# Spreading the places of the split weight strips by 32 bytes in a decoder-layer kernel

## The chip, the cores and the metric

One core of one Trainium2 chip runs the whole kernel. The metric is the device time of one execution in microseconds; the time before is the median of three runs.

## The reference

One decoder layer on 1024 tokens of width 1024, all in float32: a feed-forward half-step, a mixer with three branches, a second feed-forward half-step, each with a norm before and after. Cut to the matrix products that fill the time:

```python
f1 = swiglu(rms_norm(h, ffn1_pre_g), ffn1_w_in, ffn1_w_out)      # 1024 -> 2 x 2816 -> 1024
h = h + 0.5 * rms_norm(f1, ffn1_post_g)
u = rms_norm(h, mix_pre_g)
p_rwkv, p_swa, q_mem, gate_logits = split(u @ w_in)              # 1024 -> 1792 + 768 + 512 + 3072
y_a, y_b, y_c = rwkv7_mix(...), sliding_window_gqa(...), memory_cross_attention(...)
merged = g_a * (y_a @ w_branch[0]) + g_b * (y_b @ w_branch[1]) + g_c * (y_c @ w_branch[2])
h = h + rms_norm(merged @ w_out, mix_post_g)
f2 = swiglu(rms_norm(h, ffn2_pre_g), ffn2_w_in, ffn2_w_out)
return h + 0.5 * rms_norm(f2, ffn2_post_g)
```

## The kernel before

Activations lie feature-major: 128 features on the partitions, 512 tokens (one half) along them, in tiles of 2048 bytes per partition. A product of two float32 numbers is made of three matmuls in the type float32r: each operand is split into a rounded part, hi, and the rest, lo, and mm3 adds hi x hi, hi x lo and lo x hi in PSUM. The weight is the operand that is loaded into TensorE (stationary), the activations stream past it (moving). Every matmul comes with a weight load of its own, also where two that follow each other use the same weights.

The weights come in strips, in the order of a list that plan() writes. Half a strip is four blocks of 128 x 128, 2048 bytes per partition. raw() sends the DMA of a half into one of five w_raw buffers; operand() makes w_hi of it on ScalarE (a cast) and w_lo on VectorE (a subtraction). In the feed-forward input layers the halves are also added and subtracted first (w_sum and the raw buffers in operands()), since these layers use a scheme with fewer products on sums of blocks. prefetch() runs this eight operands ahead of the matmuls, at a raised priority; a recording layer orders the instructions of each engine by readiness and priority, and the DMAs of the weights keep their program order on SyncE's queue. For the last strips of the second feed-forward layer, operand() takes a pool of its own, keep.

w_hi and w_lo each have eight buffers (OPS) of 2048 bytes. Where they lie follows from the pools: the constants end at byte 17632 of a partition, the five raw buffers at 27872; the eight hi places start at 27872 + 2048 i, the eight lo places at 44256 + 2048 i. Divided by 512 all sixteen leave the remainder 224. The blocks inside a place are 512 bytes apart. The moving operands: the u tiles start at 163808 + 2048 i, the f and r tiles at 108512 + 2048 i, all with remainder 480; the y tiles of the last branch (line 379 and 380 write them) at 60640 + 2048 i, remainder 224; the keep pool's places have remainder 480. Of the float32 matmuls outside mm3, mkv against mem_g have remainders 224 and 224 (line 1023), bones against m 480 and 256 (line 820).

The lines of mm3 are 317, 318 and 319; operand()'s cast is line 254 and its subtraction 256. px, py, pz, po, pgate, pr, pq, pb and pw name PSUM tiles by what they hold; px, py and pz are those of the feed-forward inputs.

Of the kernel before, what the change touches and what calls it, by code (L numbers as in the profile page):

```python
# [11 lines left out]
F32R = mybir.dt.float32r  # L12
# [5 lines left out]
P = 128  # L18
# [17 lines left out]
OPS = 8  # L36
# [164 lines left out]
class Builder:  # L201
# [4 lines left out]
    def plan(self):  # L206
        seq = []
        for f in ("ffn1", "ffn2"):
            items = [(f + "_gate", j) for j in range(FIRST[f])] + [(f + "_rest", j) for j in range(FIRST[f])]
            items += [(f + "_pair", j) for j in range(FIRST[f], KF)]  # L210
            items += [(f + "_out", q) for c in OUT_STRIPS for q in c]

            items += [(f + "_out", q) for q in OUT_STRIPS[-1]] * (f == "ffn1")
            if f == "ffn1":
                seq += items
                first = [("win", f) for f in MIX_FIRST]
                seq += first + [("win", f) for f in FILL] + first
                seq += [("win", f) for p in range(NPAIR) for f in (8 + p, 4 + p, p) if f not in MIX_FIRST]
                seq += [("win", j) for j in ATT_BLOCKS]
                seq += [("win", 24 + g) for g in range(24)]  # L220
                seq += [("wb", 4 * i + q) for i in BRANCHES + BRANCHES[2:] for q in range(4)]
                seq += [("wout", o) for o in range(KD)] * 2
            else:
                seq += items
        self.seq = seq
        self.raws = []
        for name, i in seq:
            f, _, kind = name.partition("_")
            if kind in ("gate", "rest", "pair"):
                self.raws += [(f + "_in", i)] + [(f + "_in", i + KF)] * (kind != "gate")  # L230
            else:
                self.raws.append((name, i))
        self.raw_pos, self.raw_ready = 0, []
        self.lead, self.urgent = 300, 1000
        self.op_base = self.op_use = self.op_pos = 0
        self.ops_ready = []
        self.gen = self.operands()

    def raw(self, ahead):
# [9 lines left out]
        return self.raw_ready.pop(0)  # L249

    def operand(self, x, pool=None):
        pool = pool or self.wpool
        hi = pool.tile([P, 4, P], F32R, tag="w_hi", name="w_hi", bufs=OPS)
        self.nc.scalar.copy(hi, x)  # L254
        lo = pool.tile([P, 4, P], F32R, tag="w_lo", name="w_lo", bufs=OPS)
        self.nc.vector.tensor_tensor(lo, x, hi.bitcast(F32), ALU.subtract)  # L256
        return hi, lo

# [1242 lines left out]
```

## Time and profile before

| | |
|---|---|
| median of three runs | 2378.07 us (2376.53 to 2379.35) |
| the profiled execution | 2381.53 us, span 2379.8 us |
| mean granted TensorE clock | 0.996 |
| HBM read and written | 231.41 and 89.13 MB |

By stage (windows of the span, busy us of the engine in it):

| us | what runs | PE | DVE | ACT |
|---|---|---|---|---|
| 0 to 200 | start, first part of ffn1's input layer | 189.56 | 156.61 | 84.91 |
| 200 to 460 | rest of it | 260.00 | 146.54 | 98.20 |
| 460 to 790 | ffn1's output layer, first projections | 328.21 | 213.95 | 117.85 |
| 790 to 1220 | the recurrence and projections beside it | 427.40 | 304.06 | 156.90 |
| 1220 to 1530 | attention, gates, branches | 305.65 | 169.66 | 142.55 |
| 1530 to 1680 | last branch, output projection | 146.53 | 99.68 | 59.16 |
| 1680 to 2100 | ffn2's input layer | 419.06 | 304.61 | 163.13 |
| 2100 to 2380 | ffn2's output layer and the end | 267.48 | 148.32 | 68.94 |

A row of the profile names the line, the engine, the operation, and output <- inputs with buffer numbers left out; PE is a matmul, PEld a weight load. Busy time of PE counts overlapping matmuls once. A row of the timeline gives start and duration in us. A row of windows gives the stretch, its length, busy us (and instructions) by engine in the order PE, PEld, DVE, ACT, POOL where they occur, the granted clock, the DMA share and GB/s. A row of waits says who waited for whom: us in total, times, the longest.

### The profile page before, as it was taken

The numbers are of one execution on the slowest core, as the hardware profiler recorded it, in microseconds if no ns is written. First come the engines' busy times: TensorE is split into PE (matmuls) and PEld (weight loads), VectorE is DVE, ScalarE is ACT, GpSimd is POOL, SyncE is SP. The second block draws the span as 40 slices with busy tenths as digits, with TensorE's granted clock in tenths as the row PEclk, the third lists the DMA queues.
The fourth block names the chain that finished last, engine by engine and source line by source line (L and its number), as shares of the span: only waits on it lengthen the run. The fifth ranks groups of instructions, "written<-read, shape, count | busy, mean of one in ns | idle before, by whom it ended". The sixth has DMA issues, their size and how long they took to land.

```text
span 2379.8 us, 33514 instructions
## 1 busy us (share of the span) xinstructions
PE 2343.9 (98%) x12388; PEld 1916.1 (81%) x12388; DVE 1543.4 (65%) x2584; ACT 891.6 (37%) x1648; POOL 95.5 (4%) x134
## 2 busy tenths in 40 slices
PE   8999999999999999999999999999999999999998
PEld 6788888888888777888868887778888888878888
DVE  6986555655478776894655456475998765564535
ACT  5423333422345444223454455234652233342211
POOL 0000000000000000001310000240000000000000
PEclk9999999999999999999999999999999999999999
DMA  7453222533244325325444324555545432263303
GB/s 277 136 188 121 86 87 80 178 115 106 97 161 142 110 99 189 135 93 175 144 156 153 123 97 150 185 188 166 174 162 183 156 120 82 83 202 100 114 23 107
DMA packets 196195, 323.80 MB, mean 136 GB/s; under 512 B 35360, under 2 KB 65568, under 8 KB 195776
## 3 DMA queue, kind: packets, MB, share of 16 engines
q1 hardware_dynamic: 180000, 294.33, 37.7%
q10 hardware_dynamic: 16032, 27.33, 3.4%
q8 instruction: 98, 1.61, 0.3%
q14 instruction: 65, 0.53, 0.1%
HBM read 231.41 MB, written 89.13 MB: 135 GB/s over the span
## 4 chain that ended last, share of the span: by engine, by line
PE 89%; DVE 5%; DMA 3%; ACT 2%; issue 1%; ACTq 0%; SPq 0%; DVEq 0%
PE po L317 7%; PE po L318 6%; PE po L319 6%; PE px L317 6%; PE px L318 6%; PE px L319 6%; PE pgate L317 4%; PE pgate L319 4%; PE pgate L318 4%; PE pz L317 3%; PE pz L318 3%; PE pz L319 3%; PE pr L319 2%; PE pr L317 2%; PE pr L318 2%; PE pb L318 2%
## 5 line engine op out<-in xcount | busy, mean ns | idle before, releaser
L254 ACT CAST w_hi<-w_raw 128x512 fp32r<-128x512 f32 x544 | 336.6, 621 | 903.0 <-PE po L318 213.1
L256 DVE TENSOR_TENSOR w_lo<-w_raw,w_hi 128x512 fp32r<-128x512 f32 x544 | 381.5, 702 | 183.0 <-ACT w_hi L254 171.7
L317 PE MATMUL po<-u,w_hi 128*128 128x512 f32 (+1 forms) x768 | 285.9, 372 | 0.9 <-DVE acc L627 0.9
L318 PE MATMUL po<-u,w_hi 128*128 128x512 f32 (+1 forms) x768 | 285.3, 372 | 0.0
L319 PE MATMUL po<-u,w_lo 128*128 128x512 f32 (+1 forms) x768 | 285.3, 372 | 0.0
L630 DVE TENSOR_TENSOR acc<-po,acc 128x512 f32<-128x512 f32 (+1 forms) x136 | 89.6, 658 | 162.6 <-PE po L319 162.0
L317 PEld LDWEIGHTS po<-u,w_hi 128*128 128x128 f32 x768 | 144.7, 188 | 26.3 <-DVE acc L627 1.6
L318 PEld LDWEIGHTS po<-u,w_hi 128*128 128x128 f32 x768 | 144.7, 188 | 24.9
L319 PEld LDWEIGHTS po<-u,w_lo 128*128 128x128 f32 x768 | 144.7, 188 | 25.0
L317 PE MATMUL pgate<-u,w_hi 128*128 128x512 f32 x384 | 152.8, 398 | 0.0
L319 PE MATMUL pgate<-u,w_lo 128*128 128x512 f32 x384 | 151.8, 395 | 0.0
L318 PE MATMUL pgate<-u,w_hi 128*128 128x512 f32 x384 | 150.0, 391 | 0.0
L317 PE MATMUL px<-f,w_hi 128*128 128x512 f32 x352 | 137.6, 391 | 3.1 <-ACT u L543 0.9
L317 PE MATMUL px<-u,w_hi 128*128 128x512 f32 x352 | 137.3, 390 | 1.2 <-ACT vm L1110 0.9
L318 PE MATMUL pz<-u,w_hi 128*128 128x512 f32 x352 | 137.2, 390 | 0.2 <-DVE u L380 0.2
L319 PE MATMUL px<-u,w_lo 128*128 128x512 f32 x352 | 137.2, 390 | 0.0
L317 PE MATMUL pz<-u,w_hi 128*128 128x512 f32 x352 | 137.0, 390 | 0.1
L319 PE MATMUL pz<-u,w_lo 128*128 128x512 f32 x352 | 137.0, 389 | 0.0
L318 PE MATMUL px<-u,w_hi 128*128 128x512 f32 x352 | 137.0, 389 | 0.0
L318 PE MATMUL px<-f,w_hi 128*128 128x512 f32 x352 | 136.9, 389 | 0.0
L319 PE MATMUL px<-f,w_lo 128*128 128x512 f32 x352 | 136.9, 389 | 0.0
L389 ACT ACTIVATE sq<-acc 128x512 f32<-128x512 f32 (+1 forms) x104 | 61.0, 598 | 93.2 <-DVE acc L630 75.7
(314 smaller groups left out, 4665.7 us busy)
## 6 DMA issues: line engine op xcount, KB each, us to landing
w_raw<-in_ffn_in SPq DMA_DIRECT2D x220, 256.0 KB
w_raw<-in_win SPq DMA_DIRECT2D x112, 256.0 KB
w_raw<-in_ffn_out SPq DMA_DIRECT2D x104, 256.0 KB
hid_d<-g SPq DMA_DIRECT2D x88, 256.0 KB
hid<-hid_d SPq DMA_DIRECT2D x88, 256.0 KB
gate_d<-gate SPq DMA_DIRECT2D x24, 512.0 KB
pk_d<-pk ACTq DMA_DIRECT2D x4, 2560.0 KB
f<-pk_d SPq DMA_DIRECT2D x16, 640.0 KB
```

What stands on the lines that cost most here:

```text
L254: self.nc.scalar.copy(hi, x)
L256: self.nc.vector.tensor_tensor(lo, x, hi.bitcast(F32), ALU.subtract)
L317: mm(out, wh, xh, start=first, stop=False, **kw)
L318: mm(out, wh, xl, start=False, stop=False, **kw)
L319: mm(out, wl, xh, start=False, stop=last, **kw)
L389: nc.scalar.activation(sq, x, ACT.Square)
L630: self.nc.vector.tensor_tensor(out, ps, out, ALU.add)
```

## The change

Each of the sixteen places gets a buffer name of its own, with one buffer of 4 x 128 + 8 numbers, 2080 bytes, of which the first 2048 are used. plan() asks for all of them at the start, hi first, so that they lie one behind the other; operand() takes them in turn (place), hi and lo together, ahead of the cast. The keep pool goes on as it was.

```diff
+        self.place = 0
+        for t in ("hi", "lo"):
+            for i in range(OPS):
+                self.wpool.tile([P, 4 * P + 8], F32R, tag=f"w_{t}{i}", name=f"w_{t}", bufs=1)
...
     def operand(self, x, pool=None):
-        pool = pool or self.wpool
-        hi = pool.tile([P, 4, P], F32R, tag="w_hi", name="w_hi", bufs=OPS)
+        if pool:
+            hi, lo = (pool.tile([P, 4, P], F32R, tag="w_" + t, name="w_" + t, bufs=OPS) for t in ("hi", "lo"))
+        else:
+            hi, lo = (
+                self.wpool.tile([P, 4 * P + 8], F32R, tag=f"w_{t}{self.place}", name=f"w_{t}", bufs=1)[:, : 4 * P].rearrange("p (k c) -> p k c", c=P)
+                for t in ("hi", "lo")
+            )
+            self.place = (self.place + 1) % OPS
         self.nc.scalar.copy(hi, x)
-        lo = pool.tile([P, 4, P], F32R, tag="w_lo", name="w_lo", bufs=OPS)
         self.nc.vector.tensor_tensor(lo, x, hi.bitcast(F32), ALU.subtract)
```

In the built program the hi places now start at 17632 + 2080 i and the lo places at 34272 + 2080 i: remainders 224, 256, 288, 320, 352, 384, 416, 448 and 480, 0, 32, 64, 96, 128, 160, 192. The raw buffers lie behind them at 50912 + 2048 i (remainder 224, as before). Everything behind in the left part of the memory moves up by 512 bytes; the u, f, r and hid tiles, which are laid from the right, stay.

The number of instructions of each engine is unchanged. Their order differs at three places: the first pairs of ffn1's input layer, a few projections of the mixer, and the first pairs of ffn2's input layer. ScalarE's queue in the first pairs of ffn1, before (w_sum and w_raw are the sources of the split, u and f parts of the moving operands, g the gate):

```order
L254 CAST w_hi<-w_raw 128x512
L254 CAST w_hi<-w_sum 128x512
L379 CAST u<-acc 128x512
L254 CAST w_hi<-w_raw 128x512
L379 CAST f<-t 128x512 x3
L254 CAST w_hi<-w_raw 128x512 x2
L558 ACTIVATE g<-g 128x512 x2
L254 CAST w_hi<-w_raw 128x512
L254 CAST w_hi<-w_sum 128x512
```

and in the changed program (ten lines were added above, so that line 254 is 265, 379 is 389, 558 is 568):

```order
L265 CAST w_hi<-w_raw 128x512
L389 CAST u<-acc 128x512
L389 CAST f<-t 128x512
L265 CAST w_hi<-w_sum 128x512
L389 CAST f<-t 128x512 x2
L265 CAST w_hi<-w_raw 128x512 x2
L568 ACTIVATE g<-g 128x512
L265 CAST w_hi<-w_sum 128x512
L265 CAST w_hi<-w_raw 128x512 x4
```

The first split of w_sum comes later by two casts of moving operands, the second one earlier by one split and one activation. TensorE's queue at the same place, where groups of two pairs are interleaved (mm3's lines 317 to 319 are 327 to 329 in the changed program), before:

```order
L317 MATMUL px<-f,w_hi 128x512
L319 MATMUL px<-u,w_lo 128x512
L317 MATMUL px<-u,w_hi 128x512
L318 MATMUL px<-u,w_hi 128x512
L318 MATMUL px<-f,w_hi 128x512
L319 MATMUL px<-f,w_lo 128x512
L317 MATMUL px<-f,w_hi 128x512
```

and in the changed program:

```order
L327 MATMUL px<-f,w_hi 128x512 x2
L328 MATMUL px<-f,w_hi 128x512
L329 MATMUL px<-f,w_lo 128x512
L328 MATMUL px<-f,w_hi 128x512
L329 MATMUL px<-f,w_lo 128x512
L327 MATMUL px<-f,w_hi 128x512 x2
L328 MATMUL px<-f,w_hi 128x512 x2
```

The groups on u that stood between those on f have moved behind them; the matmuls are the same ones.

## The prediction

> **What bounds the kernel now.** I read the page first: how busy each engine is, and what the chain that ended last is made of.
>
> ```profile
> PE 2343.9 (98%) x12388; PEld 1916.1 (81%) x12388; DVE 1543.4 (65%) x2584; ACT 891.6 (37%) x1648; POOL 95.5 (4%) x134
> PE 89%; DVE 5%; DMA 3%; ACT 2%; issue 1%; ACTq 0%; SPq 0%; DVEq 0%
> ```
>
> TensorE is busy for 98% of the span and holds 89% of the chain. Next I asked for three stretches: the first 24 us, the last 14 us, and what lies between.
>
> ```profile
> 24.00:2366.00 2342.00, 2323.97 (x12301) 1899.00 (x12301) 1526.03 (x2535) 876.74 (x1622) 92.61 (x125) 1.00 0.41 134
> ```
>
> Between the two ends TensorE idles 2342.00 - 2323.97 = 18.0 us in all, at a granted clock of 1.00. So a change pays only if it alters the pace of the matmul stream itself; all stalls together are 18 us. The pace is read from the timeline, in a stretch with no stall, for a 512-column matmul on split weights and its weight loads, and later for the 256-column ones at the end:
>
> ```profile
> 299.66 0.39 PE L319 MATMUL py<-r,w_lo 128*128 128x512 f32 x1
> 299.89 0.39 PE L317 MATMUL py<-r,w_hi 128*128 128x512 f32 x1
> ...
> 301.93 0.39 PE L317 MATMUL px<-u,w_hi 128*128 128x512 f32 x1
> 299.89 0.19 PEld L318 LDWEIGHTS py<-r,w_hi 128*128 128x128 f32 x1
> 300.12 0.19 PEld L319 LDWEIGHTS py<-r,w_lo 128*128 128x128 f32 x1
> 2329.74 0.28 PE L319 MATMUL po<-u,w_lo 128*128 128x256 f32 x1
> ...
> 2331.18 0.28 PE L319 MATMUL po<-u,w_lo 128*128 128x256 f32 x1
> ```
>
> Columns are start, duration, engine, line, operation. The 0.39 is the latency of one matmul; they overlap, and the pace is the distance between starts. From 299.66 to 301.93 lie ten steps: 227 ns each. From 2329.74 to 2331.18 lie twelve: 120.0 ns each. So 256 more columns cost 107 ns, 0.417 ns a column; 512 columns are 213.4 ns, and **13.3 ns per matmul are fixed**, whatever its width. Each weight load (0.19 us) starts when the matmul ahead of it starts and is over before the next one is due. Whether the fixed part has to do with where the weights lie is the whole question.
>
> **The change part by part.** *The offsets.* All matmuls on split strips are at the three lines of mm3:
>
> ```profile
> 0.00:2380.00 2380.00, 1194.27 (x3088) 580.24 (x3088) 1.00 0.41 136
> 0.00:2380.00 2380.00, 1189.19 (x3088) 580.31 (x3088) 1.00 0.41 136
> 0.00:2380.00 2380.00, 1193.72 (x3088) 580.43 (x3088) 1.00 0.41 136
> ```
>
> These are the windows over the whole span for lines 317, 318 and 319 alone: 3 x 3088 = 9264 matmuls, each with a load. Their fixed part is 9264 x 13.3 ns = 123 us, 5.2% of the time. That is the most any placement could win, and each ns on all of them is 9.3 us.
>
> Before, all sixteen places leave the remainder 224 when the address is divided by 512, and the u, f and r tiles leave 480: the distance is 256 everywhere. The y tiles of the last branch, though, lie at remainder 224, a distance of 0. Their pace:
>
> ```profile
> 1565.77 0.39 PE L317 MATMUL pb<-y,w_hi 128*128 128x512 f32 x1
> ...
> 1567.13 0.39 PE L317 MATMUL pb<-y,w_hi 128*128 128x512 f32 x1
> ```
>
> Six steps in 1.36 us, 227 ns: the same. Within a strip the four blocks lie 512 bytes apart and run evenly through the rows of 299.66 to 301.93, so no multiple of 256 matters. What the trace lacks for these operands is a distance that is an odd multiple of 32. It has them for plain F32 matmuls, seen by their loads:
>
> ```profile
> L1023 PE MATMUL pq<-mkv,mem_g 128*128 128x512 f32 x32 | 14.1, 595 | 0.0
> 25.10 0.19 PEld L1023 LDWEIGHTS pq<-mkv,mem_g 128*128 128x128 f32 x1 [0.24 <-issue]
> ...
> 27.25 0.19 PEld L1023 LDWEIGHTS pq<-mkv,mem_g 128*128 128x128 f32 x1 [0.24 <-issue]
> 812.88 0.19 PEld L820 LDWEIGHTS rk<-m,bones 128*128 128x128 f32 x1 [0.24 <-issue]
> 813.31 0.19 PEld L820 LDWEIGHTS rk<-m,bones 128*128 128x128 f32 x1 [0.24 <-issue]
> 813.74 0.19 PEld L318 LDWEIGHTS pr<-u,w_hi 128*128 128x128 f32 x1 [0.24 <-issue]
> ```
>
> The mkv product is 16 matmuls in the program and 32 records here, so each record streams its columns twice: 5 steps in 2.15 us are 430 ns, which is 2 x 213.4 and 3 ns more. There weights and moving operand lie 0 apart. For rk<-m,bones they lie 288 apart (480 against 256; nine times 32), and the steps are 430 ns again. So where an odd distance can be seen, it costs and saves nothing. It is no proof: an F32 record takes twice as long for its columns, so its reads may have room that the split operands lack.
>
> Bounds: if nothing is read at a worse moment, 0; if the fixed part falls to the F32 rows' 3 ns on all matmuls, 9264 x 10.3 ns = 95 us faster; if all take the slowest undisturbed steps of this trace, dearer. I find those where the stream follows other matmuls:
>
> ```profile
> 814.40 0.19 PEld L317 LDWEIGHTS pr<-u,w_hi 128*128 128x128 f32 x1
> 814.63 0.19 PEld L318 LDWEIGHTS pr<-u,w_hi 128*128 128x128 f32 x1
> 814.87 0.19 PEld L319 LDWEIGHTS pr<-u,w_lo 128*128 128x128 f32 x1
> ```
>
> Steps of 235 ns, 8 above the steady 227: 9264 x 8 = 74 us slower. Between -95 and +74 I take **0**, since every distance that the rows do show, two for the split operands and an even and an odd one for F32, gives the same pace.
>
> The Trainium skill bears on the fixed part twice. "TensorE: Matmul & The Clock Gate", in its step-by-step part, says that loading the next weights takes no read bandwidth from the running matmul, since the two have ports of their own; by that rule no distance matters. The F32 rows agree (3 ns), the 13.3 ns need another reason. Its section "Back-to-back issue gap" gives N/2.4 + 2.5, 216 ns for 512 columns; by that figure 11 ns x 9264 = 101 us would be there to win. [...]
>
> *The writes into the places.*
>
> ```profile
> L254 ACT CAST w_hi<-w_raw 128x512 fp32r<-128x512 f32 x544 | 336.6, 621 | 903.0 <-PE po L318 213.1
> L256 DVE TENSOR_TENSOR w_lo<-w_raw,w_hi 128x512 fp32r<-128x512 f32 x544 | 381.5, 702 | 183.0 <-ACT w_hi L254 171.7
> ```
>
> The same casts and subtractions write into shifted places. Were each a tenth dearer (34 and 38 us), it would hide behind matmuls: ACT idles 903 us and DVE 183 us ahead of exactly these. I take 0.
>
> *The order.* No instruction is added or removed. With places of their own the scheduler puts the split of w_sum ahead of other splits in the first pairs of both feed-forward layers, and in ffn1 a block of three-matmul groups (f before u) moves with it. What can be won there is what stands idle:
>
> ```profile
> 100.00:170.00 70.00, 68.54 (x295) 54.53 (x295) 60.39 (x97) 23.06 (x41) 3.06 (x9) 1.00 0.51 164
> PE px L317 <- DVE u L541: 0.7, 2, 0.4
> PE px L317 <- ACT w_hi L254: 0.7, 2, 0.4
> 1790.00:1880.00 90.00, 89.54 (x395) 73.48 (x394) 70.26 (x112) 26.06 (x44) 0.00 (x0) 1.00 0.50 163
> ```
>
> The idle time is 1.46 us in ffn1's first pairs and 0.46 in ffn2's: at most 1.9 us faster. For a loss, a split that slips behind one other comes 0.62 + 0.70 = 1.3 us late; on each of the six pairs or so that the rows touch, it is 8 us. DVE is busy for 60.39 of 70 us there, so some slip is likely, yet the split moved forward is waited for as well; I take 0 and keep -2 to +8. If a split comes late, what waits is PE's next px group, and behind it the whole stream.
>
> *The size.* 512 bytes per partition more move the pools above by 512, a multiple of all that the distances above are counted in: 0.
>
> **Sum.** The profiled execution took 2381.5 us (span 2379.8 and 1.7 around it); 0 + 0 + 0 leaves it there. It is 3.5 us above the median of the three runs, 2378.07, so I forecast **2378 us** as a median, no change.
>
> **The rivals.**
>
> *The equal distance is what costs the 13.3 ns (faster).* For it: the fixed part is there although each load ends before its matmul, it is 4 times the F32 rows', and the one distance class is common to all places. Against: the y rows and the odd F32 rows. If half of the sixteen new distances were free, 9264/2 x 10.3 = 48 us: 2330; if all but one, 2290.
>
> *Some new distances collide (slower).* The loads run in step with the moving stream (rows at 299.89), so a shift of 32 bytes could put both onto the same part of the memory for the whole load. At half of the places and 8 ns, 37 us: 2415. It decides from one place in eight upward (9264/8 x 8 ns = 9 us). For it: nothing in the trace has tried such distances. Against: the F32 rows.
>
> *The order bites (slower).* The splits pulled forward delay the sums that the next pair needs: +5 to +8 us, 2384 to 2386.
>
> *The change doesn't do what it says.* It does: in the built program the hi places leave remainders 224, 256 ... 448 and the lo places 480, 0, 32 ... 192, sixteen different ones, against 480 of the u tiles. Only the operands of the last kept strips, in a pool of their own, stay as they are.
>
> **How the numbers follow.** About 0.2% (4.8 us) is what a measurement of this kernel can tell from no change. No change of pace: 0.52; faster by distance 0.24; collisions 0.16; order 0.08. The first case holds 2374 to 2383 and spills 0.02 to either side. Faster: 0.24 + 0.02 = 0.26. Within 0.2%: 0.48. Slower: 0.16 + 0.08 + 0.02 = 0.26. The likeliest case's own range is 2374 to 2383. For 8 in 10 the range must take in about half of both pace cases: down to 2328, just beyond the half-free case, and up to 2412, near the half-colliding one.
>
> **What would show it.** Right: steps of 227 and 120 ns in the same stretches, at every place; 18 us of idle time, give or take 3; the windows 100 to 170 and 1790 to 1880 with under 3 us of idle time more. Wrong by the first rival: steps below 227 ns that repeat with a period of eight strips' halves. By the second: steps above 227 with that period, and PE still 98% busy. By the third: waits of px for w_hi or w_lo above 2 us in the first pairs. The forecast is wrong as soon as steps differ between places by more than 0.5 ns on average.

## The result, and the profile after

The changed kernel takes **2415.9 us** (2414.35 to 2416.97, three runs) against 2378.07: 1.0156 times the time before, 95% interval 1.0142 to 1.017. The profiled execution took 2416.97 us, span 2415.2. One execution of e3, an experiment below, took 4759.84 us, about twice as long as the others; no run shows why, and e3's figures are those of its other three.

The page of the changed kernel: busy time by engine, and the chain that ended last (lines 317 to 319 of mm3 are 327 to 329 now).

```profile
PE 2385.2 (99%) x12388; PEld 1918.1 (79%) x12388; DVE 1544.4 (64%) x2584; ACT 894.7 (37%) x1648; POOL 95.6 (4%) x134
PE 92%; DVE 3%; DMA 2%; ACT 2%; issue 1%; DVEq 0%; ACTq 0%; SPq 0%
```

TensorE is busy for 41.3 us more with the same 12388 matmuls; the other engines have not changed by 4 us. The windows of the changed kernel, between the two ends and at the two places where the order changed (stretch, length, busy us and instructions of PE, PEld, DVE, ACT, POOL, granted clock, DMA share, GB/s):

```profile
24.00:2401.50 2377.50, 2365.08 (x12302) 1900.80 (x12302) 1526.90 (x2534) 879.76 (x1622) 92.70 (x125) 1.00 0.40 132
100.00:170.00 70.00, 69.08 (x295) 54.70 (x295) 60.28 (x97) 24.26 (x41) 3.19 (x9) 1.00 0.50 163
1813.00:1905.00 92.00, 92.00 (x398) 74.44 (x397) 71.08 (x113) 24.79 (x41) 0.00 (x0) 1.00 0.49 163
```

The waits of TensorE in ffn1's first pairs, and the groups that write into the places:

```profile
PE px L327 <- DVE u L551: 0.6, 1, 0.6
PE px L327 <- ACT w_hi L265: 0.3, 1, 0.3
```

```profile
L265 ACT CAST w_hi<-w_raw 128x512 fp32r<-128x512 f32 x544 | 337.2, 621 | 924.6 <-PE po L328 217.9
L266 DVE TENSOR_TENSOR w_lo<-w_raw,w_hi 128x512 fp32r<-128x512 f32 x544 | 381.4, 703 | 196.1 <-ACT w_hi L265 183.8
```

The two waits come to 0.9 us, against 1.4 before, and the splits take what they took. The idle time went down, from 18.0 to 2377.50 - 2365.08 = 12.4 us, and in the first pairs from 1.46 to 0.92 and from 0.46 to 0. The clock is the same. So the time was lost in the pace of the stream itself. The timeline of TensorE in the changed kernel (start, duration in us):

```profile
290.57 0.39 PE L329 MATMUL pz<-u,w_lo 128*128 128x512 f32 x1
290.80 0.39 PE L327 MATMUL px<-f,w_hi 128*128 128x512 f32 x1
...
293.07 0.39 PE L328 MATMUL px<-f,w_hi 128*128 128x512 f32 x1
293.30 0.40 PE L329 MATMUL px<-f,w_lo 128*128 128x512 f32 x1
293.53 0.39 PE L327 MATMUL pz<-u,w_hi 128*128 128x512 f32 x1
...
296.09 0.39 PE L329 MATMUL pz<-u,w_lo 128*128 128x512 f32 x1
296.32 0.40 PE L327 MATMUL px<-f,w_hi 128*128 128x512 f32 x1
...
298.89 0.39 PE L329 MATMUL px<-f,w_lo 128*128 128x512 f32 x1
```

Twelve matmuls use one pair of places. From 290.57 to 293.30 twelve steps take 2.73 us, 227.5 ns each; from 293.30 to 296.09 they take 2.79, 232.5 each; from 296.09 to 298.89 2.80, 233.3 each. The pace changes with the last matmul on the old place (293.30): that is the one under which the first weights of the next place are loaded.

The same in numbers of matmuls, in 260 us of ffn1 without a stall, before and then after:

```profile
200.00:460.00 260.00, 260.00 (x1149) 215.36 (x1148) 146.54 (x226) 98.20 (x167) 0.00 (x0) 1.00 0.28 94
```

```profile
200.00:460.00 260.00, 260.00 (x1123) 210.62 (x1122) 143.25 (x221) 94.29 (x159) 0.00 (x0) 1.00 0.25 86
```

1149 matmuls went through before, 1123 now. This row is the quickest way to read the pace and stands below for other kernels too.

Every matmul of the trace can be matched to the program, and so to the addresses of its moving operand and of the weights whose load runs beneath it, those of the next matmul. Mean steps of 512-column matmuls on split weights in the changed kernel, by the moving operand's address less that of the weights loaded beneath it, modulo 256 (steps of stalls, over 300 ns, left out; a thousand or more steps each):

```
distance     0     32     64     96    128    160    192    224
mean ns  227.2  233.2  230.0  233.6  232.2  233.6  233.2  233.1
```

All together the 8683 such steps average 231.98 ns, against 227.02 before (8685): 8683 x 4.96 ns = 43 us more. Less idle time gives 18.0 - 12.4 = 5.6 back; 37 are left, and the profiled executions differ by 35.4, the medians by 37.8. These are means: at the distance 96, for instance, the steps under which a lo part is loaded average 236.6 ns and the others 232.1.

### The profile page after: what moved, and what is told of

It is laid out like the page before. It is cut to its first block, busy times and chain, and to the rows that moved or that the text cites. A ratio compares the mean times of both kernels' runs of the same rounds, so it can differ in the third digit from the quotient of the medians.

```text
span 2415.2 us, 33504 instructions
## 1 busy us (share of the span) xinstructions
PE 2385.2 (99%) x12388; PEld 1918.1 (79%) x12388; DVE 1544.4 (64%) x2584; ACT 894.7 (37%) x1648; POOL 95.6 (4%) x134
## 4 chain that ended last, share of the span: by engine, by line
PE 92%; DVE 3%; DMA 2%; ACT 2%; issue 1%; DVEq 0%; ACTq 0%; SPq 0%
PE po L327 7%; PE po L328 7%; PE po L329 7%; PE px L327 6%; PE px L328 6%; PE px L329 6%; PE pgate L327 4%; PE pgate L329 4%; PE pgate L328 3%; PE pz L328 3%; PE pz L329 3%; PE pz L327 3%; PE pr L329 2%; PE pr L327 2%; PE pr L328 2%; PE pb L328 2%
## 5 line engine op out<-in xcount | busy, mean ns | idle before, releaser
L327 PE MATMUL po<-u,w_hi 128*128 128x512 f32 (+1 forms) x768 | 288.7, 376 | 0.8 <-DVE acc L637 0.8
L328 PE MATMUL po<-u,w_hi 128*128 128x512 f32 (+1 forms) x768 | 288.5, 376 | 0.0
```

The costliest lines, as they stand in the source:

```text
L327: mm(out, wh, xh, start=first, stop=False, **kw)
L328: mm(out, wh, xl, start=False, stop=False, **kw)
```

## The experiments

Theory 1: the step between two matmuls depends on the distance of the moving operand to the weights that are loaded beneath it, modulo 256 bytes. Rivals: the order and the buffer names; the weights' own address; the mixture of offsets.

**Own names without the 32 bytes (e1).**

```diff
-self.wpool.tile([P, 4 * P + 8], F32R, tag=f"w_{t}{i}", name=f"w_{t}", bufs=1)
+self.wpool.tile([P, 4 * P], F32R, tag=f"w_{t}{i}", name=f"w_{t}", bufs=1)
```

> The sixteen places keep buffer names of their own, asked for in the same order, but without the 32 bytes: all distances from the moving operand to the places are multiples of 256 again, as before. Theory 1 (the step between matmuls depends on the distance between the moving operand and the weights that are loaded beneath it, counted modulo 256 bytes): steps of 227 ns everywhere, a time of 2376 to 2381 us. Rival, order and names: the time stays near that of the change, 2410 to 2418 us, with idle time of TensorE or waits for w_hi and w_lo.

2381.19 us, 1.0013 times before (1.0003 to 1.0022). Every engine has the instructions of the changed kernel in the very same order. So names and order cost 0.13%, some 3 us, at most 0.22%, and the 32 bytes the rest.

**The moving operands 96 bytes lower (e2), the left part 96 higher (e3), both (e4).** All are made from the kernel before; e2 adds the first line, e3 the second, e4 both, with 160 bytes on the left.

```diff
+outer.enter_context(tc.tile_pool(name="pads", bufs=1, side="right")).tile([P, 24], F32, name="pad_right")
 self.upool = outer.enter_context(tc.tile_pool(reuse_waits="tile", name="u", bufs=32, side="right"))
...
+cp.tile([P, 24], F32, name="pad_left")
 self.vecs = cp.tile([P, NVEC], F32, name="vecs")
```

> The kernel before, with its places where they were, but every tile that is laid from the right (u, f, r, hid: the moving operands) 96 bytes lower: 8987 of 9179 matmuls then stream at a distance of 160 modulo 256 from the weights loaded beneath them. Theory 1: steps of about 233.6 ns, as the changed kernel has at this distance, so 8987 x 6.6 ns = 59 us more than before, 2437 us (2425 to 2445). Rival 2 (the weights' own address counts, remainders other than 224 being bad): the weights have not moved, 2378 us.

> The kernel before, with everything that is laid from the left (constants, raw buffers, places, pools) 96 bytes higher and the moving operands where they were: the same distance of 160 for the same 8987 matmuls as with the moving operands 96 lower, at other addresses of both. Theory 1: the same time as that run within 0.3%, about 2437 us. Rival 2: slower as well, but by what the address alone costs, so not the time of that run, which stays at 2378 us by it. If mixed distances are what costs (a rival 3: it is the change of offset from place to place, not the offset), 2378 us here and there.

> The kernel before with both moved: the left part 160 bytes higher, the moving operands 96 lower. Every address of weights and of moving operands leaves another remainder modulo 256 than before, and the distance is again a multiple of 256. Theory 1: steps of 227 ns and 2376 to 2381 us. Rival 2: slower, since the places' remainder is no longer 224: 2395 us or more.

e2 2429.7 us, ratio 1.0216 (1.0199 to 1.0233); e3 2428.4, ratio 1.0211 (1.0194 to 1.0228); e4 2379.53, ratio 1.0003 (0.9994 to 1.0013). In e2 the places stand where they always stood, and it is 50 us slower; in e3 the moving operands do, and it is as slow; in e4 both have new addresses and the old distance, and nothing is lost. The same window of 260 us, first of e2, then of e3, then of e4:

```profile
200.00:460.00 260.00, 260.00 (x1111) 209.00 (x1111) 141.46 (x219) 92.37 (x157) 0.00 (x0) 1.00 0.24 83
```

```profile
200.00:460.00 260.00, 260.00 (x1111) 209.01 (x1110) 141.37 (x220) 92.40 (x157) 0.00 (x0) 1.00 0.24 83
```

```profile
200.00:460.00 260.00, 260.00 (x1149) 215.29 (x1148) 146.77 (x227) 97.93 (x166) 0.00 (x0) 1.00 0.27 93
```

1111, 1111 and 1149 matmuls. So a changed distance is enough, whichever side is moved, with one distance for all; neither address by itself is it, and a mixture is not needed. The distance sets the mean and not every step: of the 512-column steps of the kernel before 93% are 226 or 227 ns, while nearly all of e2's at 160 lie between 230 and 238. The expected 2437 us was 7 too high, though the steps at 160 were longer than in the changed kernel (mean 234.3 ns): as there, part of the extra time took the place of stalls. Between the two ends TensorE idles 11.0 us in e2, against 18.0 before.

**The hi places alone, 64 bytes apart (e5).**

```diff
-self.wpool.tile([P, 4 * P + 8], F32R, tag=f"w_{t}{i}", name=f"w_{t}", bufs=1)
+self.wpool.tile([P, 4 * P + 16 * (t == "hi")], F32R, tag=f"w_{t}{i}", name=f"w_{t}", bufs=1)
```

> The changed kernel with the padding on the hi places alone, 64 bytes each, none on the lo places: of 9179 loads that follow a split matmul, 4726 lie at a multiple of 256, 1486 at 64, 1481 at 128 and 1486 at 192. With the mean steps that the changed kernel has at these distances (227.0, 230.0, 232.2, 233.2 ns) theory 1 adds 1486 x 3.0 + 1481 x 5.2 + 1486 x 6.2 ns = 21 us of matmul time; in the two runs with the distance 160 about 0.82 of such a sum arrived in the time, so 2397 us (2392 to 2402). Rival (what costs is that neighbouring loads have different offsets, not the distance): two thirds of the loads change offsets against their neighbours, so two thirds of the change's 37 us or more, 2404 us or above, with steps above 227 at the distance 0 too.

2409.49 us, ratio 1.0134 (1.0117 to 1.0151): above what the table gives, and where the rival had it, with steps above 227 at the distance 0 too, as it said. So theory 1, with the load beneath alone, is not the whole account. Steps by the distance of the load before and the load beneath:

```
before, beneath    0,0    64,0   64,64   128,0   128,128   192,0   192,192
mean ns          228.1   233.3   230.5   232.5     232.5   229.7     235.3
```

A load at distance 0 after one at 64 costs 233 ns, not 227. So where distances alternate within the three matmuls of a block, the load before counts as well; how it does so was not tested. In the changed kernel hi and lo of a place have the same distance (their places are 16640 bytes apart, 65 times 256), which hid this: there the mixture comes once in twelve matmuls.

**One distance for all (e6, e9, e10, e11).** The kernel before with a left pad of 192, 32, 128 and 224 bytes.

> The kernel before with everything laid from the left 192 bytes higher: a distance of 64 for 8987 loads, of 0 for 192. Theory 1: steps of about 230 ns as the changed kernel has at 64, 27 us of matmul time, some 22 of them in the time, 2401 us (2394 to 2408). Against 160, with 50 us: the step depends on which multiple of 32, not on being a multiple of 256 or not. Rival (all distances but multiples of 256 cost alike): 2429 us.

> The kernel before with everything laid from the left 32 bytes higher: a distance of 224 for 8987 loads. With the changed kernel's mean step at 224 (233.1 ns) the matmuls take 55 us more, of which about 0.82 arrive: 2423 us. If a part of the changed kernel's mean comes from the mixture of distances (a load after one at another distance pays as well, as in the run with hi places 64 apart), the uniform distance is cheaper: between 2384 and 2415 us.

> The same with 128 bytes: a distance of 128. By the changed kernel's mean step (232.2 ns) 47 us more matmul time, 2416 us; with a part of it from the mixture 2384 to 2410 us. A uniform distance under 227 ns a step, and so a time under 2375 us, would make it the version that beats both; none of the theories expects it.

> The same with 224 bytes: a distance of 32. By the changed kernel's mean step (233.3 ns) 57 us more, 2424 us; with a part of it from the mixture 2384 to 2415 us.

```
distance          0 (before)    32      64     128     160     224
run                             e11      e6     e10   e2,e3      e9
mean step ns        227.0    233.3   229.1   232.6   234.3   233.4
time us                     2420.24  2391.75 2418.52  2429.7  2423.62
ratio                        1.0175   1.0057  1.0168  1.0216   1.0189
interval, from               1.0146   1.0042  1.0138  1.0199   1.0160
to                           1.0205   1.0072  1.0197  1.0233   1.0219
```

The window of 260 us of e6, e9, e10 and e11:

```profile
200.00:460.00 260.00, 260.00 (x1138) 213.34 (x1137) 144.79 (x224) 97.33 (x165) 0.00 (x0) 1.00 0.27 92
```

```profile
200.00:460.00 260.00, 260.00 (x1116) 209.33 (x1115) 142.21 (x221) 93.45 (x158) 0.00 (x0) 1.00 0.24 84
```

```profile
200.00:460.00 260.00, 260.00 (x1120) 210.83 (x1119) 142.53 (x220) 94.10 (x159) 0.00 (x0) 1.00 0.24 86
```

```profile
200.00:460.00 260.00, 260.00 (x1116) 208.79 (x1115) 141.97 (x220) 93.17 (x158) 0.00 (x0) 1.00 0.24 84
```

Each of the five distances has a mean step (512 columns) within 1 ns of what the changed kernel has at the same distance, so little of the change's loss came from its mixture of places. 64 costs least (1138 matmuls), where the expected 2401 us was 9 too high. The "cheaper" of the other expectations did not come: 2418 to 2424 us, within 4 us of the 2423, 2416 and 2424 reckoned from the changed kernel's means. No mean is below 227 ns, and no version beats the kernel before. In each of these runs, and in e2 and e3, some 97 steps load weights of the keep pool, 256 bytes further from the moving operand; their means differ from the run's other steps by 0.3 ns at most. That, and the 227 ns at both 0 and 256 in the kernel before, is what the modulo 256 rests on.

**Distances that are no multiple of 32 (e7, e8).** The changed kernel with the strips 16 and 24, or 4 and 28 bytes into their places (offsets in numbers of 4 bytes: 4 and 6 in e7, as shown, 1 and 7 in e8).

```diff
-[:, : 4 * P].rearrange("p (k c) -> p k c", c=P) for t in ("hi", "lo")
+[:, s : s + 4 * P].rearrange("p (k c) -> p k c", c=P) for t, s in (("hi", 4), ("lo", 6))
```

> The changed kernel with the strips 16 bytes (hi) and 24 bytes (lo) into their places: distances 16, 48, 80 ... 240 for the hi loads and 8, 40, 72 ... 232 for the lo loads, none a multiple of 32. It asks whether the step at a multiple of 256 is the least there is. Theory 1 with a period of 256 and no finer structure: steps between 229 and 238 ns at all of them, the time near the changed kernel's 2416 us (2405 to 2430). A second form of it (the fixed 13.3 ns of the kernel before are themselves a collision at distance 0): some distance close to 0 or 256, that is 8, 16 or 240, shows steps under 225 ns.

> The same with 4 bytes (hi) and 28 bytes (lo): distances 28, 60 ... 252 for the hi loads and 4, 36 ... 228 for the lo loads. If lines of 16 or 32 bytes are what is met, 252 and 4 (one number off a multiple of 256) stand near 227 ns or a few ns above, and the others near their neighbours at multiples of 32; if a start off such a line costs a further read, all are a few ns above them and the time passes 2425 us. Second form of theory 1: 252 or 4 under 225 ns.

One execution each: 2416.39 and 2419.87 us. Mean steps at 512 columns lie between 229.6 (distance 4) and 237.3 ns (196) at all 32 distances; none is under 227. Here hi and lo have unequal distances, so the mixture is in these means, and they are no curve of the distance alone.

**One column for all (e12).**

```diff
 (wh, wl), (xh, xl) = w, x
+wh, wl = (t[:, 0:1].broadcast_to([P, P]) for t in (wh, wl))
```

> The kernel before, except that each of the 9264 split matmuls takes one column of its weights 128 times instead of the 128 columns (the products are therefore others). The load then reads 4 bytes of a partition where it read 512, with the same number of instructions and of streamed columns. If the fixed 13.3 ns of a step come from the load's reads beside the stream, the step at 512 columns falls below 224 ns, towards 213.4 plus the 3 ns of the F32 rows, and the time by up to 95 us, towards 2285 us. If they come with any load, whatever it reads, it stays at 227 ns and 2378 us.

One execution: 2405.71 us, mean step 230.8 ns at 512 columns, longer and not shorter. Both expectations fall. At this width the step with a load that takes the same 4 bytes of a partition 128 times is longer than the one with a load that reads 512 bytes at distance 0. At 256 columns it is shorter, 115.5 ns against 120.2 (means of 376 steps each). The window of that kernel:

```profile
200.00:460.00 260.00, 260.00 (x1138) 213.43 (x1137) 145.43 (x225) 96.21 (x163) 0.00 (x0) 1.00 0.26 90
```

So at 512 columns it is not how much a load reads that sets the step. It fits that the place it reads at each moment, against the place the stream is at, decides, but that was not shown by itself, and the load's repeated column may cost something of its own.

## Why the prediction was wrong

**The bound** was right: only the pace of the stream could move this kernel, and it did.

**The offsets** is the step that failed: "I take 0, since every distance that the rows do show, two for the split operands and an even and an odd one for F32, gives the same pace." Two inferences in it did not hold. The two distances of the split operands, 256 and 0, are one and the same modulo 256, so they were no test. And the F32 matmuls at an odd distance, 430 ns as the even ones, say nothing of the split operands; the text named the reason (they take twice as long for their columns, so there is room) and then used them all the same. In place of the 0 stand 43 us of matmul time; the bound of +74 held it.

**The size of the rival.** Collisions at half of the places and 8 ns were 37 us and 2415; measured were 37.8 and 2415.9. That the distance between load and stream costs time is what the runs show; that the two then meet on the same part of the memory, as the rival had it, is not shown. The agreement of the number is half chance: seven of the eight distances cost, at 3 to 6.5 ns each, 5 ns on the mean. It got 0.16, and the range was cut at 2412, 3 us short of the price that the text itself had worked out.

**The faster rival** falls with e2 to e11 for the 512-column matmuls: there the distance 0 has the shortest mean step of all that were run. None of the 95 us that the text held possible came. For the few 256-column ones, the last section says, other distances are indeed quicker.

**The rule of the Trainium skill** on ports of their own for load and stream ("TensorE: Matmul & The Clock Gate", the step-by-step part) does not hold for these operands: a load at another distance lengthens the 512-column step that it runs under, from 227 to 234.3 ns at 160.

**The writes** cost no time that shows, as said: the cast of a split strip takes 621 ns as before and the subtraction 703 against 702.

**The order**: -2 to +8 us, taken as 0; e1 has it at 3 us (0.7 to 5.2).

**The sum's translation** from steps into time was left out of the forecast: idle time shrank by 5.6 us under the longer steps.

## What to carry to other kernels

Where every matmul loads its weights while the one before streams, and nothing else holds TensorE up, the relative place of weights and moving operand in memory was worth 0.6 to 2.2% of the time here. Tiles of 2048 bytes laid without padding were already at the best distance that was tried for 512-column matmuls in float32r; no other type was tried. A pad of a few bytes in front of a pool, constants for instance, can move it by accident: 32 bytes cost 1.9% in e9. So the distance modulo 256 is worth looking at. And a row is only evidence for values that differ in the quantity at issue: count the classes first.

## What the runs showed of the hardware that was not expected

At 512 columns the mean step depends on the distance modulo 256 bytes: 227 ns at 0, 229.1 at 64, up to 234.3 at 160, and it also depends on the load before (227 or 233 ns at the same distance 0).

What a step takes beyond the stream of its columns is not one amount for both widths, except at the distance 0. At distance 64 the 256-column matmuls of e6 run faster than those of the kernel before (timeline of TensorE in e6):

```profile
2341.80 0.28 PE L319 MATMUL po<-u,w_lo 128*128 128x256 f32 x1
...
2343.92 0.28 PE L319 MATMUL po<-u,w_lo 128*128 128x256 f32 x1
```

Eighteen steps in 2.12 us are 117.8 ns against 120.0, while the 512-column ones of the same kernel take 229.1 against 227. Every run with one distance other than 0 agrees: the means of its 375 or so 256-column steps are 116.7 (e11), 117.8 (e6), 117.9 (e3), 118.6 (e9 and e10) and 119.2 ns (e2), against 120.2 before. So the distance that is best at 512 columns is the dearest of these at 256, where a step is shorter than a load's own 0.19 us. And e2 and e3, both at 160, differ there by 1.3 ns, so at this width the distance alone does not settle the step. No fixed addition to the stream, the same at both widths, stands behind the step; why distance 0 gives an even 13.3 ns at both stays open.
